# Value products of the first six token tiles taken from rows without the root of the norm, which a column out of PSUM applies afterwards

## The chip, the core and the metric

The kernel runs on one core of one Trainium2 chip. The metric is the device time of one execution in microseconds; the kernel before takes 2457.29 us, the median of three runs (2456.39 to 2457.72).

## What is computed

One layer of a hybrid encoder over 1088 tokens (1024 of a prompt and 64 of a running stream). The part that matters here is its beginning:

```python
xn = _rmsnorm(x, p['norm_mix_w'])
proj = xn @ p['w_in']
z, xbc, dt_raw, q, k, v, gate_ssm, gate_att = jnp.split(proj, ...)
...
def _rmsnorm(x, w):
    xf = x.astype(jnp.float32)
    y = xf * lax.rsqrt(jnp.mean(xf * xf, axis=-1, keepdims=True) + NORM_EPS)
    return (y * w.astype(jnp.float32)).astype(x.dtype)
```

The norm divides each token's row of 1024 numbers by the root of its mean square (a factor of the token) and multiplies it by a weight (a factor of the column). The projections `v` and `dt_raw` are taken first, then `q`, and the rest.

## The kernel before, in words

Activations lie transposed: features over the 128 partitions, in KT = 8 blocks, tokens along the free axis. Tokens go in nine tiles of 128 (the last of 64), and three neighbouring tiles make one part of `xn` (384, 384 and 320 tokens). Every product is taken in three matmuls of a rounded format, since a number is split into a high part (a cast, on ScalarE, ACT) and a low part (the difference, on VectorE, DVE): high x high, high x low, low x high. So a product over 1024 features is 8 x 3 = 24 matmuls.

The stage that is changed norms the nine tiles and takes the first half of the value products from them (two halves `f` of 256 columns, each with 16 columns of `dt`). Its steps for tile `x`: `fetch` loads the rows (`xc`); `squares` and `add_squares` square them and add eight blocks to two (`ns8`, shown as `ns` in the trace); `mean_square` lets TensorE (PE) sum over the partitions with a matrix of ones, which leaves each token's sum in all 128 partitions (`st`); `rstd_put` takes the root (three steps on ACT, two on DVE, into `nrs`); `weighted` and `scaled` multiply the rows by the negated weight and by `nrs`, which carries the other minus sign (`xr`); `put_high` and `put_low` write the parts `xn_hi` and `xn_lo`; `value_tile` takes the 24 products for one half into PSUM, evicts them with a copy on ACT (`vo`), stores them, and adds the bias of `dt` on DVE.

The order is set in two ways. What goes through `put` is chained by hand: each such instruction is issued after the one before it in the same engine's queue. The rest is ordered by the scheduler, within priorities. Value weights come in four blocks, two for each half, and are split on ACT and DVE as they land (`split_high`, `split_low`). For tile 0 the squares come first, `idle_products` keep PE busy with matmuls of ones in the meantime (9, then 8), then the mean, the root, the scaling and the split, and last the products. From tile 1 on `normed(x)` runs a tile ahead of the products.

Behind the stage come the projections `heads` with `project` (per block of 128 columns 24 matmuls for each of the three parts of `xn`; weights split by `weights`, line 147 and 148), and `steps`, which works on the `dt` columns on DVE and then takes sums with matmuls (lines 540 to 553).

Of the kernel before, what the change touches and what calls it, by code (L numbers as in the profile page):

```python
# [12 lines left out]
ALU = mybir.AluOpType  # L13
# [36 lines left out]
IDLE = (9, 8)  # L50
# [25 lines left out]
def hybrid_layer(ctx: ExitStack, tc: tile.TileContext, xT, xN, prm, cst, rope, wvd, win, wbs, wba, wout, wup, wdn,  # L76
# [181 lines left out]
    def value_tile(f, i, w2, dt=None, start=load, produce=product):  # L258
        m = 256 if dt is None else 272
# [3 lines left out]
        produce(ps, [(hi[:, k], lo[:, k], w2[k // 4][0][:, k % 4], w2[k // 4][1][:, k % 4]) for k in range(KT)])  # L263
        vo = staged("vo")[:, :256]
        with tc.high_priority(quick or ahead):
            S.copy(vo[:n], ps[:, :256])
            start(out=v[P * i : P * i + n, 256 * f : 256 * (f + 1)], in_=vo[:n])
            if dt is not None:
                V.tensor_tensor(out=dt[:n, i, 16 * f : 16 * f + 16], in0=ps[:, 256:],
                                in1=par[:n, O_DTB + 16 * f : O_DTB + 16 * f + 16], op=ALU.add)  # L270

    def values(f):
        w2 = [weights(win[B_V + 2 * f - 4 + u], 4, 256) for u in range(2)]
        for i in range(9):
            value_tile(f, i, w2)
            yield

    V.memset(dtw[TS:, 8], 0.0)
    with tc.tile_pool(name="nx", bufs=1) as nx:
# [21 lines left out]
        def tiles(x):  # L301
            for d, name, shape in ((s8, "ns8", [P, KT, P]), (xr, "xr", [P, KT, P]), (rs, "nrs", [P, P])):
                d[x] = nx.tile(shape, F32, name=name, tag=name, bufs=2)[..., : NORM[x]]
# [52 lines left out]

        def normed(x):
            rstd_put(x, ps[x])
            y = x + 1 if x + 1 < len(NORM) else None
            if y:  # L360
                tiles(y)
                for h in halves:
                    squares(y, h)
            if x == 1:
                scaled_half(x, halves[0])
                scaled(x, range(4, KT))
            else:
                scaled(x)
# [9 lines left out]
        def in_turns(*turns):  # L378
            turns = [(u, k) for u, ks in turns for k in ks]

            def produce(acc, terms):
                for i, (u, k) in enumerate(turns):
                    a_hi, a_lo, b_hi, b_lo = terms[k]
                    put(PE, PE.matmul, acc, a_lo if u == 2 else a_hi, b_lo if u == 1 else b_hi, start=i == 0,
                        stop=i == len(turns) - 1)

# [10 lines left out]
        xs.append(fetch(1))  # L397
        w += [raw_weights(wvd[2], 4, 272, extra), raw_weights(wvd[3], 4, 272, first)]
        w2 = [t[1:] for t in w]
        xs.append(fetch(2))  # L400
        load(out=par[:, O_FFN:], in_=prm[:, O_FFN:])
        tiles(0)
        tiles(1)
        a, b = halves
        all_k, low_k, high_k = range(KT), range(4), range(4, KT)
        idle_products(IDLE[0])
        squares(0, a)
        put(V, V.tensor_tensor, out=s8[0][:, b], in0=xs[0][:, b], in1=xs[0][:, b], op=ALU.mult)
        add_squares(0)
        ps = {0: mean_square(0, 2, put)}  # L410
        idle_products(IDLE[1])
        put(V, V.tensor_scalar_mul, par[:, O_MIX : O_MIX + KT], par[:, O_MIX : O_MIX + KT], -1.0)
        weighted(0, range(5), V)
        weighted(0, range(5, KT), S)
        rstd_put(0, ps[0])
        split_high(w[0])
        for h in halves:
            scaled_half(0, h)
            put_high(0, h)
        split_low(w[0])  # L420
        for h in halves:
            put_low(0, h)
        split_high(w[1])
        split_low(w[1])
        for h in halves:
            squares(1, h)
        add_squares(1)
# [3 lines left out]
        weighted(1, low_k, S)  # L431
        value_tile(0, 0, w2[:2], dtw, S.dma_start, in_turns((0, all_k), (1, low_k), (2, all_k), (1, high_k)))
        ps[1] = mean_square(1, 2, put)
        normed(1)
        with tc.issue_after(queue[S].ins):
            value_tile(1, 0, w2[2:], dtw, S.dma_start, in_turns((0, all_k), (2, all_k), (1, all_k)))
        for x in range(2, len(NORM) + 1):
            if x + 1 < len(NORM):
                xs.append(fetch(x + 1))
            if x < len(NORM):  # L440
                normed(x)
            for f in range(2):
                value_tile(f, x - 1, w2[2 * f : 2 * f + 2], dtw, S.dma_start, *[in_turns((0, all_k), (1, all_k), (2, all_k))] * (x == 2 and f == 0))
            if x == 3:
                load(out=con, in_=cst)
                for i, j, by in ((O_FFN, O_CW, -1.0), (O_CW, O_SN, 0.5), (O_SN, O_D, -0.5), (O_QN, O_FW, -1.0)):
                    put(V, V.tensor_scalar_mul, par[:, i:j], par[:, i:j], by)
# [3 lines left out]
    with tc.tile_pool(name="qk", bufs=1) as qk:  # L451
# [17 lines left out]
        def heads(blk0, wcol, to, plain):  # L469
# [3 lines left out]
            def block(j):  # L473
# [11 lines left out]
                return project(win[blk0 + j], evac)  # L485
# [1080 lines left out]
```

## Time and profile before

| what | value |
|---|---|
| median of three runs | 2457.29 us |
| profiled execution | 2457.47 us |
| its span on the core | 2455.7 us |
| PE, PE weight loads | 2426.9, 2351.5 us busy |
| DVE, ACT, GpSimd | 1600.6, 1137.8, 658.2 us busy |
| first value product, first projection product | 10.80, 73.51 us |

The profile is of one execution. A row of its timeline gives start, duration, engine, line, operation, output and inputs, the number of merged instructions, and in brackets the idle time ahead and what ended it. PEld is the loading of a matmul's fixed operand, PE the matmul itself, whose end is modelled. SP and ACT can issue DMAs. The span is the time from the first instruction to the last; the profiled execution is 1.8 us longer than its span.

### The profile page before, as it was taken

What the parts mean: (1) busy time and instruction counts of PE and PEld (TensorE: products, weight loads), DVE (VectorE), ACT (ScalarE), POOL (GpSimd) and SP (SyncE); (2) the same over time, 40 slices, a digit from 0 to 9 for tenths busy, and PEclk for the clock granted to TensorE, in tenths of its full rate; (3) what the DMA queues carried; (4) which work ended last, traced back from release to release, by engine and by line L of the source; (5) the groups of instructions that cost most, each with busy time, mean ns of one, the idle gap of its engine ahead of it and who ended that gap; (6) DMA issues with size and microseconds to landing.
All of it is one profiled execution on the core that took longest, in us unless ns stands there. A gap on an engine that the chain in (4) does not pass through costs nothing. (4 is left out here: it accounts for less than half of the span.)

```text
span 2455.7 us, 44603 instructions
## 1 busy us (share of the span) xinstructions
PE 2426.9 (99%) x16956; PEld 2351.5 (96%) x16956; DVE 1600.6 (65%) x2755; ACT 1137.8 (46%) x2497; POOL 658.2 (27%) x696
## 2 busy tenths in 40 slices
PE   9999999999999999999999999999999999999999
PEld 8999999999999999998899989999999999999999
DVE  7425254865777667546767785655776777777775
ACT  6334343644565555437664653224543434353441
POOL 0000000100011001004343333103376666655435
PEclk9999999999999999999999999999999999999999
DMA  4218158554353453345689765656234343467875
GB/s 173 82 57 293 58 216 257 139 166 129 118 162 110 129 169 106 97 159 183 201 266 323 224 197 178 191 176 189 70 117 147 116 153 116 133 209 205 223 176 163
DMA packets 269319, 403.55 MB, mean 164 GB/s; under 512 B 33296, under 2 KB 202000, under 8 KB 268976
## 3 DMA queue, kind: packets, MB, share of 16 engines
q1 hardware_dynamic: 258432, 385.06, 49.3%
q0 software_dynamic: 4608, 8.91, 2.4%
q10 hardware_dynamic: 6064, 6.72, 0.8%
q8 instruction: 133, 2.18, 0.4%
q14 instruction: 82, 0.67, 0.1%
HBM read 267.04 MB, written 133.56 MB: 163 GB/s over the span
## 5 line engine op out<-in xcount | busy, mean ns | idle before, releaser
L154 PE MATMUL mm<-xn_hi,w_hi 128*128 128x384 f32 (+1 forms) x1416 | 470.4, 332 | 0.9 <-DVE zr L590 0.9
L156 PE MATMUL mm<-xn_hi,w_lo 128*128 128x384 f32 (+1 forms) x1416 | 469.3, 331 | 0.5 <-DVE w_lo L148 0.5
L155 PE MATMUL mm<-xn_lo,w_hi 128*128 128x384 f32 (+1 forms) x1416 | 469.2, 331 | 0.0
L154 PEld LDWEIGHTS mm<-xn_hi,w_hi 128*128 128x128 f32 x1416 | 267.3, 189 | 4.8 <-issue 1.6
L156 PEld LDWEIGHTS mm<-xn_hi,w_lo 128*128 128x128 f32 x1416 | 267.4, 189 | 3.8 <-issue 2.0
L155 PEld LDWEIGHTS mm<-xn_lo,w_hi 128*128 128x128 f32 x1416 | 267.4, 189 | 2.6 <-issue 1.6
L148 DVE TENSOR_TENSOR w_lo<-w_f,w_hi 128x1024 fp32r<-128x1024 f32 x116 | 145.1, 1252 | 114.0 <-ACT w_hi L147 113.7
L1228 PE MATMUL mx<-n,wh 128*128 128x272 f32 x1076 | 206.2, 289 | 3.0 <-ACT u L1369 1.8
L1228 PE MATMUL mx<-m,w_hi 128*128 128x272 f32 x1010 | 192.3, 288 | 1.1 <-DVE down L1383 1.0
L147 ACT CAST w_hi<-w_f 128x1024 fp32r<-128x1024 f32 x116 | 121.3, 1048 | 145.8 <-PE mm L155 85.5
L1228 PEld LDWEIGHTS mx<-n,wh 128*128 128x128 f32 x1076 | 169.0, 188 | 4.1 <-ACT u L1369 2.5
L1228 PEld LDWEIGHTS mx<-m,w_hi 128*128 128x128 f32 x1010 | 158.7, 188 | 1.8 <-DVE down L1383 1.5
L1228 PE MATMUL mx<-n,wl 128*128 128x272 f32 x538 | 155.5, 289 | 0.0
L154 PE MATMUL mm<-b_hi,w_hi 128*128 128x384 f32 (+1 forms) x448 | 145.9, 327 | 0.8 <-DVE b_g L211 0.6
L156 PE MATMUL mm<-b_hi,w_lo 128*128 128x384 f32 (+1 forms) x448 | 145.0, 325 | 0.6 <-DVE w_lo L148 0.6
L1228 PE MATMUL mx<-m,w_lo 128*128 128x272 f32 x505 | 145.5, 288 | 0.0
L155 PE MATMUL mm<-b_lo,w_hi 128*128 128x384 f32 (+1 forms) x448 | 145.0, 324 | 0.0
L708 ACT ACTIVATE p_t<-sc,mx 128x1024 f32<-128x1024 f32 (+5 forms) x144 | 106.1, 738 | 78.9 <-DVE mx L699 37.2
L619 DVE SCALAR_TENSOR_TENSOR cc<-pre,par,cc 128x384 f32<-128x384 f32 (+1 forms) x216 | 126.5, 586 | 19.5 <-ACT cc L617 14.3
L607 POOL COPY pre<-pre 128x3 f32<-128x3 f32 x48 | 13.2, 276 | 456.9 <-ACT pre L608 346.8
L1019 ACT CAST w_hi<-ws 128x512 fp32r<-128x512 f32 (+1 forms) x62 | 37.6, 607 | 147.3 <-PE mx L1228 101.4
L154 PE MATMUL mx<-xn_hi,w_hi 128*128 128x384 f32 (+1 forms) x312 | 104.8, 336 | 0.8 <-DVE zr L590 0.8
(417 smaller groups left out, 6626.9 us busy)
## 6 DMA issues: line engine op xcount, KB each, us to landing
w_f<-in_win_dram SPq DMA_DIRECT2D x76, 512.0 KB, 4.0
w_f<-in_wup_dram SPq DMA_DIRECT2D x44, 512.0 KB, 3.8
hr<-q_sc SPq DMA_DIRECT2D x70, 272.0 KB, 4.8
bc<-a_sc SPq DMA_DIRECT2D x32, 512.0 KB, 5.8
q_sc<-hb SPq DMA_DIRECT2D x44, 272.0 KB, 2.3
gb<-q_sc SPq DMA_DIRECT2D x44, 272.0 KB, 3.8
x_sc<-cc SPq DMA_DIRECT2D x48, 192.0 KB, 2.3
q_sc<-gb SPq DMA_DIRECT2D x33, 272.0 KB, 2.2
```

Of the source, the lines that this page charges most:

```text
L147: S.copy(hi, w)
L148: V.tensor_tensor(out=lo, in0=w, in1=hi, op=ALU.subtract)
L154: PE.matmul(ps, a_hi, b_hi, start=i == 0, stop=False)
L155: PE.matmul(ps, a_hi, b_lo, start=False, stop=False)
L156: PE.matmul(ps, a_lo, b_hi, start=False, stop=i == n - 1)
L607: G.tensor_copy(pre[:, 0:3], tail)
L619: V.scalar_tensor_tensor(cc[:, :m], pre[:, i : i + m], cw(i), cc[:, :m], ALU.mult, ALU.add)
L708: act(p_t[:n, :nk], sc[c][:n, :nk], AF.Exp, bias=mx[:n, c : c + 1], accum_out=dst)
L1019: S.copy(hi, src)
L1228: PE.matmul(ps, w[x][:, c], b[y][:, k], start=start and k == t == 0, stop=k == nk - 1 and t == 2, skip_group_check=not start)
```

## The change

Tiles 0 to 5 (`RAW = 6`) are no longer normed before their value products. `raw(x)` weights the rows (half on ACT, half on DVE) and splits them; the products are taken from these rows. The squares and the mean follow beside, and the mean of tile `y` stands among the products of tile `y + 1`. A matmul of one row by one column turns the root from a row into a column in PSUM (`column`), a copy on DVE brings it to SBUF (`by`), and the eviction of tile `y`'s products, held in PSUM until then, multiplies by it, since in `v` tokens lie along the partitions. Tiles 6 to 8 are normed as before, ahead of their products. At the end `again(x)` multiplies the kept rows of tiles 3, 4, 5, 0, 1, 2 by their kept roots and splits them once more into `xn`, for the projections; the first projection block takes the parts in the order 2, 1, 0. The squares of the first tile go wholly to ACT, idle products are 14 in one run in place of 9 and 8, the four weight blocks are loaded ahead of the second tile's rows, value tiles 1 and later take high x high and high x low of the low and then of the high feature blocks first, then low x high, and the value stores are issued by SP in place of ACT.

In instructions: PE gets 6 column matmuls and 3 idle ones fewer, ACT 12 casts, 15 weightings and one square of 512 more and 18 DMA issues fewer, DVE 12 low parts, 9 products of 512 by the root, 21 weightings and 6 small copies more, and 36 fused weight-and-root products and one square fewer.

```diff
-IDLE = (9, 8)
+IDLE = 14
+RAW = 6
...
-    def project(block, evac):
+    def project(block, evac, order=(0, 1, 2)):
         w_hi, w_lo = weights(block, KT, P)
-        for (c, w), (hi, lo) in zip(WIDE, xn):
+        for x in order:
+            (c, w), (hi, lo) = WIDE[x], xn[x]
...
+    def value_out(f, i, ps, dt=None, start=load, by=None):
+        n = ps.shape[0]
         vo = staged("vo")[:, :256]
         with tc.high_priority(quick or ahead):
-            S.copy(vo[:n], ps[:, :256])
+            if by is None:
+                S.copy(vo[:n], ps[:, :256])
+            else:
+                act(vo[:n], ps[:, :256], AF.Copy, scale=by[:n])
             start(out=v[P * i : P * i + n, 256 * f : 256 * (f + 1)], in_=vo[:n])
...
+                    V.scalar_tensor_tensor(out, ps[:, 256:], by[:n], bias, ALU.mult, ALU.add)
...
+        def raw(x):
+            weighted(x, range(4), S)
+            weighted(x, range(4, KT), V)
+            for h in halves:
+                put_high(x, h)
+            for h in halves:
+                put_low(x, h)
+
+        def again(x):
+            for h in halves:
+                scaled_half(x, h)
+                put_high(x, h)
+            for h in halves:
+                put_low(x, h)
...
+        for x in range(1, len(NORM)):
+            y, z = x - 1, x + 1
+            if x + 3 < len(NORM):
+                xs.append(fetch(x + 3))
+
+            def means():
+                for u in [y] * (y < RAW) + [z] * (z == RAW):
+                    ps[u] = mean_square(u, 2, put)
+
+            def column():
+                pc = stat(P)[:, 0:1]
+                put(PE, PE.matmul, pc, rs[y][0:1], ones[0:1, 0:1], start=True, stop=True)
+                by[y] = nx.tile([P, 1], F32, name="by", tag="by", bufs=2)
+                column_at[y] = pc
+
+            to = [None, None]
+            at = (24 if x == 1 else 12, means), (18, column)
+            turns = (0, low_k), (1, low_k), (0, high_k), (1, high_k), (2, all_k)
+            to[0] = value_products(x, w2[:2], 272, in_turns(*turns, at=at[0]) if y < RAW else product)
+            if z < RAW:
+                tiles(z)
+                raw(z)
+            elif z < len(NORM):
+                normed(z)
+            if y < RAW:
+                rstd_put(y, ps[y])
+            if x < RAW:
+                add_squares(x)
+            if z < RAW:
+                stats(z)
+            if z + 1 == RAW:
+                tiles(RAW)
+                stats(RAW)
+                add_squares(RAW)
+            to[1] = value_products(x, w2[2:], 272, in_turns(*turns, at=at[1]) if y < RAW else product)
+            if y < RAW:
+                put(V, V.tensor_copy, by[y], column_at[y])
+                for f in range(2):
+                    value_out(f, y, held[f, y], dtw, by=by[y])
...
+        for x in (*range(3, RAW), *range(3)):
+            again(x)
...
-                return project(win[blk0 + j], evac)
+                return project(win[blk0 + j], evac, (2, 1, 0) if blk0 == B_Q and j == 0 else (0, 1, 2))
```

The order of PE at the very start, before (`w_hi` and `w_lo` are value weights, `xn_hi0` and `xn_lo0` the parts with tile 0, `st` a bank for sums):

```order
L296 MATMUL st_153<-ones_74 128x128 [waits DVE_49]
L299 MATMUL st_153<-ones_74 128x128 x8
L299 MATMUL st_167<-ns8_147,ones_74 128x128 [waits DVE_49]
L299 MATMUL st_167<-ns8_147,ones_74 128x128
L299 MATMUL st_170<-ones_74 128x128 x8
L299 MATMUL mx_217<-w_hi_125,xn_hi0_87 128x272 [waits Activation_49]
```

And in the changed kernel:

```order
L307 MATMUL st_153<-ones_74 128x128 [waits DVE_49]
L310 MATMUL st_153<-ones_74 128x128 x13
L310 MATMUL mx_191<-w_hi_125,xn_hi0_87 128x272 [waits Activation_49]
L310 MATMUL mx_191<-w_hi_125,xn_hi0_87 128x272 x3
L310 MATMUL mx_191<-w_hi_125,xn_lo0_88 128x272 [waits DVE_49]
```

The mean of tile 0 and the idle products behind it are gone from between, and the first product waits for ACT with nothing ahead of it but one run of idle products.

The order of DVE in the changed kernel in the pass for tile 5 (`ns8_689` holds the squares of tile 7, `xr_605` and `nrs_606` rows and root of tile 6, `nrs_481` the root of tile 4, `by_741` its column):

```order
L236 SCALAR_TENSOR_TENSOR nn0_682<-st_667,nn0_682 128x128
L237 SCALAR_TENSOR_TENSOR nrs_606<-nn0_682,nn1_683 128x128
L310 SCALAR_TENSOR_TENSOR xr_605<-xc_448,par_72,nrs_606 128x128 x8
L310 TENSOR_TENSOR ns8_689<-ns8_689 128x512
L310 TENSOR_TENSOR ns8_689<-ns8_689 128x256
L310 TENSOR_TENSOR xn_lo2_92<-xr_605,xn_hi2_91 128x4x128 x2
L236 SCALAR_TENSOR_TENSOR nn0_711<-st_664,nn0_711 128x128
L237 SCALAR_TENSOR_TENSOR nrs_481<-nn0_711,nn1_712 128x128
```

The nearest piece of before, where one tile is normed at a time:

```order
L234 SCALAR_TENSOR_TENSOR nn0_492<-st_423,nn0_492 128x128
L235 SCALAR_TENSOR_TENSOR nrs_406<-nn0_492,nn1_493 128x128
L299 SCALAR_TENSOR_TENSOR xr_405<-xc_394,par_72,nrs_406 128x128 x8
L299 TENSOR_TENSOR ns8_499<-ns8_499 128x512
L269 TENSOR_TENSOR dtt_98<-mx_521,par_72 128x16
L299 TENSOR_TENSOR ns8_499<-ns8_499 128x256
L299 TENSOR_TENSOR xn_lo1_90<-xr_405,xn_hi1_89 128x4x128 x2
```

A second root, that of tile 4, now stands behind tile 6's whole chain, and PE's column for tile 4 stands behind that root.

The order of DVE ahead of the projections in the changed kernel (`w_lo_1108` is the low part of the first projection's weights; `xr_386`, `xr_480`, `xr_579` are the kept rows of tiles 3, 4 and 5):

```order
L310 TENSOR_TENSOR xr_386<-xr_386,nrs_387 128x512 x2
L279 TENSOR_TENSOR dtt_98<-mx_866,par_72 128x16
L310 TENSOR_TENSOR xn_lo1_90<-xr_386,xn_hi1_89 128x4x128 x2
L310 TENSOR_TENSOR xr_480<-xr_480,nrs_481 128x512 x2
L279 TENSOR_TENSOR dtt_98<-mx_910,par_72 128x16
L310 TENSOR_TENSOR xn_lo1_90<-xr_480,xn_hi1_89 128x4x128
L149 TENSOR_TENSOR w_lo_1195<-w_f_1193,w_hi_1194 128x1024
L310 TENSOR_TENSOR xn_lo1_90<-xr_480,xn_hi1_89 128x4x128
L310 TENSOR_TENSOR xr_579<-xr_579,nrs_580 128x512 x2
L279 TENSOR_TENSOR dtt_98<-mx_943,par_72 64x16
L149 TENSOR_TENSOR w_lo_1288<-w_f_1286,w_hi_1287 128x1024
L149 TENSOR_TENSOR w_lo_1108<-w_f_1106,w_hi_1107 128x1024
```

And before, where `w_lo_1055` is the one of the first projection:

```order
L299 TENSOR_TENSOR xn_lo2_92<-xr_770,xn_hi2_91 128x4x64 x2
L269 TENSOR_TENSOR dtt_98<-mx_868,par_72 128x16
L269 TENSOR_TENSOR dtt_98<-mx_897,par_72 128x16
L148 TENSOR_TENSOR w_lo_1142<-w_f_1140,w_hi_1141 128x1024
L269 TENSOR_TENSOR dtt_98<-mx_926,par_72 64x16
L148 TENSOR_TENSOR w_lo_1235<-w_f_1233,w_hi_1234 128x1024
L148 TENSOR_TENSOR w_lo_1055<-w_f_1053,w_hi_1054 128x1024
```

Ten operations on kept rows now stand ahead of the same three splits, and those of tiles 0, 1 and 2 behind them, ahead of `steps`. From the second half of the first projections on, at about 100 us, the order is that of before on every engine.

More of the change, by code (lines that the diff above doesn't have):

```diff
@@ L361, in normed @@
                 tiles(y)
[L362 to L368, printed above, removed]
+                stats(y)
+            scaled(x)
             if y:
@@ L430, in hybrid_layer @@
             split_low(t)
[L431 to L441, printed above, removed]
+        ps, by, held, column_at = {}, {}, {}, {}
@@ new lines, in hybrid_layer @@
+        for f in range(2):
+            held[f, 0] = value_products(0, w2[2 * f : 2 * f + 2], 272, in_turns(
+                (0, low_k), (2, low_k), (1, low_k), (0, high_k), (2, high_k), (1, high_k)))
+        tiles(1)
+        raw(1)
+        stats(1)
+        add_squares(0)
+        for x in range(1, len(NORM)):
[32 more added lines that the diff above has]
+                put(V, V.tensor_copy, by[y], column_at[y])
+                for f in range(2):
+                    value_out(f, y, held[f, y], dtw, by=by[y])
```

61 lines of the change are left out of this document (33 added, 28 removed).

## The prediction

> **What bounds the kernel now.** I read the page first, then busy time by stretch, then what TensorE waits for at the start, then the rows there one by one.
>
> ```profile
> span 2455.7 us, 44603 instructions
> ...
> PE 2426.9 (99%) x16956; PEld 2351.5 (96%) x16956; DVE 1600.6 (65%) x2755; ACT 1137.8 (46%) x2497; POOL 658.2 (27%) x696
> ```
> ```profile
> 0.00:100.00 100.00, 94.54 (x661) 91.01 (x662) 68.23 (x183) 50.87 (x111) 0.20 (x4) 1.00 0.42 146
> ```
> TensorE (PE) is busy 2426.9 of 2455.7 us, so only what it waits for, or is given more of, moves the end. The change rewrites the normalisation and value products, which fill about the first 73 us, and the order on every engine is the same again from about 100 us on. What lies behind is shifted as one block. In the first 100 us PE is idle for 5.5 us by its matmul rows and 9.0 by its weight loads (PEld). I count by the loads, since a matmul's end is modelled. The pieces of that idle time after the first value product:
>
> ```profile
> 10.80 0.55 PEld L299 LDWEIGHTS mx<-w_hi,xn_hi 128*128 128x128 f32 x4 [0.48 <-ACT xn_hi L299]
> 12.40 0.55 PEld L299 LDWEIGHTS mx<-w_hi,xn_hi 128*128 128x128 f32 x4 [1.05 <-ACT w_hi L299]
> 15.49 0.52 PEld L299 LDWEIGHTS st<-ns,ones 128*128 128x128 f32 x4 [0.54 <-PE mx L299]
> 20.40 0.55 PEld L299 LDWEIGHTS mm<-w_hi,xn_hi 128*128 128x128 f32 x4 [1.41 <-ACT xn_hi L299]
> 21.45 0.55 PEld L299 LDWEIGHTS mm<-w_hi,xn_hi 128*128 128x128 f32 x4 [0.25 <-ACT xn_hi L299]
> 27.68 0.19 PEld L154 LDWEIGHTS mx<-w_hi,xn_hi 128*128 128x128 f32 x1 [0.45 <-ACT xn_hi L299]
> 28.79 0.52 PEld L312 LDWEIGHTS st<-ns,ones 128*128 128x128 f32 x4 [0.56 <-DVE ns L299]
> ```
> The first value product starts at 10.80. Behind it PE loses 1.05 + 0.54 + 1.41 + 0.25 + 0.45 + 0.56 = 4.26 us; from 29 us on it runs without a break to the first projection product at 73.51:
>
> ```profile
> 16.92 1.07 PEld L299 LDWEIGHTS mx<-w_hi,xn_lo 128*128 128x128 f32 x8
> 17.93 1.07 PEld L299 LDWEIGHTS mx<-w_lo,xn_hi 128*128 128x128 f32 x8
> ```
> ```profile
> 48.54 0.61 PE L312 MATMUL st<-ns,ones 128*128 128x128 f32 x4
> ...
> 49.11 0.29 PE L154 MATMUL mx<-w_hi,xn_hi 128*128 128x272 f32 x1
> ...
> 73.51 0.34 PE L154 MATMUL mm<-xn_hi,w_hi 128*128 128x384 f32 x1
> ```
> Eight products take 17.93 - 16.92 = 1.01 us, 0.126 each. A mean of squares with the product behind it takes 49.11 - 48.54 = 0.57, so it adds 0.445. The stage by this count: 10.80 + 9 tiles x 48 x 0.126 (54.4) + 8 means x 0.445 (3.6) + 4.26 = 73.1, where the trace has 73.5. The count holds to 0.4 us, so I count the changed kernel in the same way.
>
> **The change part by part.** *Start.* Tile 0 no longer waits for squares, mean and root before its first product. What is then late next?
>
> ```profile
> L280 ACTq DMA_DIRECT2D par<-in_prm_dram x1: 419/419/419, 0.7 to 0.7; - x1
> ...
> DMA to landing us min/median/max: 3.1/3.1/3.1
> ```
> ```profile
> L141 SPq DMA_DIRECT2D w_f<-in_wvd_dram x1: 432/432/432, 1.6 to 1.6; - x1
> ...
> DMA to landing us min/median/max: 6.1/6.1/6.1
> ```
> ```profile
> 3.72 0.63 ACT L296 ACTIVATE ns<-xc 128x512 f32<-128x512 f32 x1 [1.25 <-DMA xc<-in_xN_dram]
> 6.47 0.99 ACT L299 ACTIVATE xr<-xc,par 128x128 f32<-128x128 f32 x3 [2.12 <-DVE par L299]
> 8.63 1.08 ACT L299 CAST w_hi<-w_f 128x1088 fp32r<-128x1088 f32 x1
> 10.13 1.22 ACT L299 CAST xn_hi<-xr 128x512 fp32r<-128x512 f32 x2 [0.42 <-DVE xr L299]
> ```
> ```profile
> 4.41 0.69 DVE L296 TENSOR_TENSOR ns<-xc 128x512 f32<-128x512 f32 x1 [3.25 <-DMA xc<-in_xN_dram]
> 6.47 1.07 DVE L299 TENSOR_SCALAR xr<-xc,par 128x128 f32<-128x128 f32 x5
> 10.62 1.28 DVE L299 TENSOR_TENSOR w_lo<-w_f,w_hi 128x1088 fp32r<-128x1088 f32 x1
> ```
> The rows of tile 0 land at 3.7 and 4.4, the parameters at 3.8; weighting (0.2 a piece on DVE, 0.3 on ACT) and the two casts (1.22) are done by about 6.2. The first weights, third in the queue as before, land at 1.6 + 6.1 = 7.8. Their cast (1.08) comes last: PE starts at 8.95 instead of 10.80, **1.85 saved**. So the DMA takes the place of the root. On ACT the other three casts follow, with two squares of 0.6 between, and are done by 13.0; on DVE the four low parts (1.28, each behind its cast) end at 10.2, 11.8, 13.3 and 14.5. PE, at 0.126 a product, needs them at 10.0, 11.8, 13.3 and 14.8, so it waits 0.3 in all and finishes tile 0 at about 15.3.
>
> *Tiles 1 to 4.* A tile takes PE 48 x 0.126 + 0.445 = 6.5, with the new column 6.6. ACT has four weightings (1.2), two casts (1.2), two squares (1.2), and two evictions and three steps of the root, whose rows stand below (0.75 and 1.1): 5.5. DVE has four weightings, low part, adds and root, 0.8 + 1.3 + 1.15 + 0.65, and three small rows: 4.3. Both are done in time, so **the waits of 4.26 become 0.3**, 4.0 saved.
>
> *Added PE work.* The mean of tile 0 now stands among the products: 0.445. Six column matmuls (one row in, 128x1 out) have no row like them. Below I set nothing, above half a mean, 0.22; I take 0.15, 0.9 for six: a tiny operand, but two changes of what PE loads. Together **1.3**. Three idle products of 17 go from a stretch in which PE waits anyway: nothing.
>
> *Tile 5, where tile 6 is normed the old way.* Here the chain gets longer. In the pass for tile 5, PE's order has the means of tiles 4 and 6 after 12 products, then 30 products, the mean of tile 7, and tile 4's column. DVE's order in between is root of 6, eight weightings, the adds of 7, low part of 6, root of 4. The same links in the trace of before:
>
> ```profile
> 46.85 0.37 ACT L266 COPY vo<-mm 128x256 f32<-128x256 f32 x1 [0.63 <-PE mm L156]
> ...
> 49.19 0.37 ACT L231 ACTIVATE nn<-st,eps_t 128x128 f32<-128x128 f32 x1 [0.58 <-PE st L312]
> ```
> ```profile
> 50.27 0.29 DVE L234 SCALAR_TENSOR_TENSOR nn<-st,nn 128x128 f32<-128x128 f32 x1 [1.22 <-ACT nn L233]
> ...
> 50.92 2.19 DVE L299 SCALAR_TENSOR_TENSOR xr<-xc,par,nrs 128x128 f32<-128x128 f32 x8
> 53.03 0.68 DVE L299 TENSOR_TENSOR ns<-ns 128x512 f32<-128x512 f32 x1
> ...
> 54.18 1.29 DVE L299 TENSOR_TENSOR xn_lo<-xr,xn_hi 128x512 fp32r<-128x512 f32 x2
> ```
> From the means' issue, 0: PE has issued both at 0.9 and reaches tile 7's mean 30 x 0.126 = 3.8 later, at 4.7. DVE can start tile 6's root 1.1 after ACT has the mean (50.27 - 49.19; about 1.1 + 1.1 = 2.2), weights from 2.9 to 5.0 (53.03 - 50.92), and has the adds (54.18 - 53.03) by 6.2: PE waits 1.5. Mean done at 6.6; the low part (two at 0.6) takes until 7.3 and tile 4's root 0.65 (50.92 - 50.27), so the column can start at 7.9: another 1.3. **2.8 added.** Before, the same chain ended in time because only one tile was in it. The later tiles have room again: PE reaches their columns after the roots.
>
> The stage: -1.85 - 4.0 + 1.3 + 2.8 = **-1.7**; the projections start near 71.4 by the count, 71.8 on the trace's scale.
>
> *Projections.* Six tiles are scaled and split again: 12 scalings and 12 low parts on DVE at 0.6 each, 14.6 us, and 12 casts on ACT. DVE reaches them after tile 8's low part, whose cast stands behind ACT's eviction of tile 6 (PE ends tile 6 at 62.5 by the count; cast and low part make it 63.7). Ahead of the low part of the first projection's weights are ten such operations (6.1) and three weight splits:
>
> ```profile
> 72.32 2.36 DVE L148 TENSOR_TENSOR w_lo<-w_f,w_hi 128x1024 fp32r<-128x1024 f32 x2 [0.46 <-ACT w_hi L147]
> ...
> 75.33 0.31 DVE L532 TENSOR_SCALAR dtt<-dtt 128x288 f32<-128x288 f32 x1 [0.51 <-ACT de L522]
> ...
> 84.44 0.09 DVE L537 MEMSET da<- 64x32 f32 x1
> 89.53 0.46 DVE L541 TENSOR_SCALAR nacum<-st 128x288 f32<-128x288 f32 x1 [5.00 <-PE st L540]
> ```
> At 1.2 a split that is 3.6, with 0.6 for small rows and hand-overs 74.0. PE needs it after three products, at 71.9, and stands: before, it had six products without that operand to bridge, now two and one that itself waits 0.2. **2.3 added.** The last three tiles' parts (7.8, with the hand-overs) then put the time-step chain, 75.33 to 84.5 in the trace, with a weight split in it at 83.4 to 93.9. Before, it had 5.0 us to spare; PE's order now has its first matmul 4.8 us later (120 products ahead of it instead of 92, at 0.17), at 93.7 by the count. **0.3 added**, and no room left. The tokens of tiles 0 to 2 are not late themselves: their low parts are there at 82.6, PE asks at 84.5.
>
> The move of the 18 value stores from ACT's to SP's queue, and the later rows, I set at nothing: next in SP's queue are row tiles with a pass to spare.
>
> Sum: -1.7 + 2.3 + 0.3 = **+0.9 us**. Of the profiled execution (2457.47, 1.8 beyond its span) that makes 2458.4; the median of the runs shown is 0.2 lower, so I forecast **2458.2**. About 0.2%, 4.9 us, is what a measurement of this kernel can tell from no change.
>
> **A rule on the clock.** PE's idle products keep it busy while it waits:
>
> ```profile
> L299 PE MATMUL st<-ones 128*128 128x128 f32 x16 | 3.6, 421 | 0.0
> ```
> ```profile
> L299 PE MATMUL st<-ones 128*128 128x128 f32 x6 | 1.0, 299 | 0.0
> ```
> In 1.5 to 5.2 us such a matmul takes 421 ns, after 9.9 us 299 and less: PE works at about half rate first, although the granted clock reads 1.00 in both. It became fast after 3.4 us of unbroken work from 6.4 on; the 4.2 us from 1.05 had not been enough. Now one run of 14 products (28 matmuls at 0.213, to about 7) is followed by 2 us of nothing. The Trainium skill, "TensorE: Matmul & The Clock Gate", Part 1, says that the array runs at half clock until one free-running window of about 3.4 us has been busy, and again after an idle window of that length. By that rule 6 us of work contain a whole window most times and the gap is too short to lose it; where the windows lie badly, the value products start at half rate. The trace agrees with the 3.4 us, and no run here shows a gap of 2 us.
>
> **The rivals.** *Cold start.* If PE is at half rate from 8.95, each such us costs 0.5, less the 0.3 it waits anyway: 3.4 to 6.8 us make 1.4 to 3.1, 2459.6 to 2461.3. For it: the first stretch of 4.2 us did not do. Against: 6 us do more. Chance 0.12.
>
> *The two late chains aren't late.* If ACT and DVE run ahead of my count, the 2.8 and 2.6 go: 2452.8, just inside no change. Both are in the fixed order with durations that repeat; 0.07.
>
> *The second split makes DVE the bound.* With no room left before the time-step chain, each 1% on the 30 us of DVE from 63.7 to 93.9 costs 0.3. The 24 hand-overs between DVE and ACT there are the doubtful part: at 0.17 us more each it is 4.1 later, 2462.3, slower by over 0.2%. For it: DVE's share is 65% already, and PE has to wait in the forecast. Against: hand-overs in the rows above are 0.05 to 0.15, which I counted. Chance 0.06.
>
> *The start doesn't move,* because the weights land later than in the old queue: 1.85 comes back, 2460.1. They stand at the same place in it; 0.03.
>
> **How the numbers follow.** The forecast, with 0.72, spans 2456.4 to 2460: columns -0.9 to +0.4, each late chain 0.4 either way, landing 0.5. With the cold start and part of the others the range is 2455.8 to 2461.5. Faster by over 0.2% needs the second rival and more: 0.03. Slower: the third, and the worst of the first: 0.08. Same: 0.89.
>
> **What would show it.** First value product at 8.9, waiting for the cast of the weights; no wait over 0.4 us from there to 45; then about 1.5 us for tile 7's adds and 1.3 for tile 4's root near 49 to 51; 2 us for the weights' low part at the first projection; under 1 us at the first matmul of the time steps. It is wrong if value products come 0.25 us apart before 15 us, or if TensorE waits in a place not named here.

## The result, and the profile after

The changed kernel takes 2460.14 us (median of 13 runs, 2455.14 to 2462.83), the kernel before 2456.47 (13 runs beside it, 2452.36 to 2459.41). The ratio is 1.0016 with a 95% interval of 1.0009 to 1.0023: 0.16% slower, 2.2 to 5.7 us, and so within the 0.2% that counts as no change here, though the interval leaves out 1 and its upper end is a little beyond 0.2%. The profiled execution took 2458.27.

The page of the changed kernel, its span and the busy time of the engines; then its first 100 us as one stretch, with TensorE's granted clock after the busy times:

```profile
span 2456.5 us, 44662 instructions
...
PE 2429.5 (99%) x16962; PEld 2355.9 (96%) x16962; DVE 1601.2 (65%) x2766; ACT 1152.0 (47%) x2525; POOL 661.7 (27%) x696
```
```profile
0.00:100.00 100.00, 93.16 (x641) 90.67 (x642) 73.86 (x189) 59.50 (x130) 0.20 (x4) 0.97 0.41 144
```

TensorE is 1.4 us less busy in that stretch (93.16, before 94.54), and **the granted clock is 0.97 where it was 1.00**. These are the two things to explain. First the waits: weight loads between 8 and 80 us with idle time ahead of them, its length and releaser in brackets (the columns at 29, 36 and 43 us, with 0.15 like the one at 22.40, are left out):

```profile
8.90 0.55 PEld L310 LDWEIGHTS mx<-w_hi,xn_hi 128*128 128x128 f32 x4 [2.17 <-ACT w_hi L310]
...
22.40 0.29 PEld L310 LDWEIGHTS st<-ones,nrs 1*128 1x128 f32 x2 [0.15 <-issue]
...
52.06 0.52 PEld L325 LDWEIGHTS st<-ns,ones 128*128 128x128 f32 x4 [1.55 <-DVE ns L310]
53.80 0.29 PEld L310 LDWEIGHTS st<-ones,nrs 1*128 1x128 f32 x2 [1.21 <-DVE nrs L237]
```
```profile
78.14 0.19 PEld L157 LDWEIGHTS mm<-xn_hi,w_lo 128*128 128x128 f32 x1 [1.71 <-DVE w_lo L149]
```

The six waits of before are gone, and the three new ones of over 1 us stand where they were forecast. Yet the first projection product, with which the stage ends, starts at 75.93 instead of 73.51. The same stretch cut into windows of 3.41 us shows why:

```profile
6.27:9.68 3.41, 1.43 (x12) 1.24 (x11) 1.47 (x3) 1.93 (x3) 0.00 (x0) 1.00 1.01 402
9.68:13.09 3.41, 3.41 (x16) 3.33 (x16) 2.95 (x3) 3.41 (x5) 0.00 (x0) 0.50 1.05 405
13.09:16.51 3.42, 3.42 (x29) 3.42 (x29) 3.33 (x9) 2.95 (x8) 0.00 (x0) 1.00 1.05 402
...
50.64:54.06 3.42, 1.06 (x7) 0.79 (x6) 3.35 (x9) 1.73 (x5) 0.00 (x0) 1.00 0.00 0
54.06:57.47 3.41, 3.41 (x17) 3.40 (x17) 3.26 (x13) 2.72 (x8) 0.00 (x0) 0.50 0.19 63
```

Read the first number behind the window's length (TensorE busy) against PEclk of the *next* row. A window in which TensorE was busy for 1.43 of 3.41 us (42%), or 1.06 (31%), is followed by one at clock 0.50, and that by one at 1.00. Each of these half-clock windows costs half its length, 1.7 us, as TensorE has work throughout. It is to be seen in single products, four to a row:

```profile
11.30 1.11 PE L310 MATMUL mx<-w_hi,xn_hi 128*128 128x272 f32 x4
12.21 1.07 PE L310 MATMUL mx<-w_hi,xn_lo 128*128 128x272 f32 x4
...
14.11 0.66 PE L310 MATMUL mx<-w_hi,xn_lo 128*128 128x272 f32 x4
14.61 0.66 PE L310 MATMUL mx<-w_lo,xn_hi 128*128 128x272 f32 x4
```

12.21 - 11.30 = 0.91 for four, 0.23 each; behind 13.1 it is 0.50 for four, 0.125 each. The second surprise is the column:

```profile
22.06 0.41 PE L310 MATMUL mm<-w_hi,xn_lo 128*128 128x272 f32 x2
22.40 0.38 PE L310 MATMUL st<-ones,nrs 1*128 1x1 f32 x2
22.71 1.02 PE L310 MATMUL mm<-w_hi,xn_lo 128*128 128x272 f32 x6
...
29.35 0.38 PE L310 MATMUL st<-ones,nrs 1*128 1x1 f32 x2
```

From one column to the next it is 29.35 - 22.40 = 6.95 us, where 6.5 was counted for a tile without one: 0.45 a column, not 0.15.

### The profile page after: what moved, and what is told of

Same layout as the page of the kernel before. It is cut to its first block, busy times and chain, and to the rows that moved or that the text cites. A ratio compares the mean times of both kernels' runs of the same rounds, so it can differ in the third digit from the quotient of the medians.

```text
span 2456.5 us, 44662 instructions
## 1 busy us (share of the span) xinstructions
PE 2429.5 (99%) x16962; PEld 2355.9 (96%) x16962; DVE 1601.2 (65%) x2766; ACT 1152.0 (47%) x2525; POOL 661.7 (27%) x696
## 4 chain that ended last, share of the span: by engine, by line
PE 90%; DMA 4%; DVE 2%; ACT 1%; issue 1%; SPq 1%; POOL 0%; DVEq 0%; POOLq 0%; ACTq 0%
PE mx L1291 18%; PE mm L157 12%; PE mm L155 12%; PE mm L156 12%; PE mm L1291 7%; PE mx L155 4%; PE mx L157 4%; PE mx L156 4%; PE po L805 3%; PE sc L758 2%; PE sc L757 1%; PE mx L1350 1%; PE pt L786 1%; DMA kl_t<-k_st 1%; PE yi L921 1%; PE ye L927 1%
## 5 line engine op out<-in xcount | busy, mean ns | idle before, releaser
L670 POOL COPY pre<-pre 128x3 f32<-128x3 f32 x48 | 13.7, 285 | 453.3 <-ACT pre L671 345.3
```

## The experiments

All but one were timed in five rounds beside the kernel before; figures like 1.0011 (1.0001 to 1.0021) are ratios to it with their 95% intervals. Where traces are compared, "lateness at 100 us" is the start of the first product after 100 us against the same product of the profiled kernel before (+3.7 us in the changed kernel).

### More idle products

```diff
-IDLE = 14
+IDLE = 20
```


> Six idle products more (20 instead of 14), which fill 1.3 us of the 2.0 us in which TensorE stands before its first value product; nothing else is changed. Theory (clock by windows): TensorE's granted clock is set in fixed windows of 3.4 us; a window of which less than half is busy is followed by one at half clock. In the changed kernel 6.3 to 9.7 is 42% busy and 9.7 to 13.1 shows 0.50; now it is about 80% busy, the clock reads 1.00 there, the products keep 0.125 us each, and 1.7 us are saved less at most 0.4 us of new waits for low parts of weights: first column at about 20.8 instead of 22.4, whole 2458.5 against 2460.1. Rival (the onset of dense products draws the throttle, whatever comes before): the stretch at 0.50 stays at 9.7 to 13.1, column at 22.4, whole unchanged at 2460.1.

The window ahead of the first products, and the next, of this kernel (columns as above):

```profile
5.43:8.85 3.42, 2.43 (x22) 2.23 (x20) 1.29 (x2) 1.56 (x3) 0.00 (x0) 1.00 0.95 327
8.85:12.26 3.41, 3.02 (x21) 2.80 (x22) 2.63 (x3) 3.41 (x6) 0.00 (x0) 1.00 1.02 402
```

With the window ahead of the products 71% busy, the clock stays at 1.00; the second half-clock window, which this edit doesn't touch, is still there (53.2 to 56.6, at 0.50). The first column comes at 21.47 instead of 22.40, although the first product started 0.28 later (9.18) and, at full speed, waits 0.28 for a low part of the weights: 1.5 us gained at that place. Whole: 1.0011 (1.0001 to 1.0021), 2459.38; the gain by ratios, about 1.2 us, is inside the two intervals. The theory's sign is in the trace, the rival is out: the products begin as densely as before, and draw no throttle. Nor does it hang on one execution: of the four traces with 14 idle products three have a half-clock window at the start (the early mean's hasn't), of the six with 20 none.

### Tile 6's mean half a pass earlier

```diff
-                for u in [y] * (y < RAW) + [z] * (z == RAW):
+                for u in [y] * (y < RAW):
                     ps[u] = mean_square(u, 2, put)
...
             def column():
...
+                if z + 1 == RAW:
+                    ps[RAW] = mean_square(RAW, 2, put)
```


> The mean of tile 6 half a pass earlier (behind tile 3's column, not beside tile 4's mean), so that root 6 no longer stands in one chain with root 4. Theory (chain order): the waits for tile 7's adds (1.55 by the weight loads) and tile 4's root (1.21) fall under 0.4 each, window 50.6 to 54.1 stays over half busy, and with it the half clock at 54.1 to 57.5 goes: 2.8 + 1.7 = 4.5 less, first projection product at 71.5 instead of 75.9; the wait for the weights' low part there stays near 1.7; whole 2455.6. Rival (DVE is the bound from there on): the projection starts 4.5 earlier and waits that much longer, 6 us, for its low part; the whole stays at 2460.1.

The same pass of this kernel, in windows, and TensorE's waits at the first projection:

```profile
48.93:52.34 3.41, 3.41 (x27) 3.27 (x27) 3.15 (x11) 2.33 (x7) 0.00 (x0) 1.00 0.00 0
52.34:55.76 3.42, 3.42 (x30) 3.42 (x29) 3.39 (x12) 2.13 (x5) 0.00 (x0) 1.00 0.23 77
```
```profile
70.94 0.19 PEld L155 LDWEIGHTS mm<-xn_hi,w_hi 128*128 128x128 f32 x1 [0.45 <-ACT w_hi L148]
72.62 0.19 PEld L155 LDWEIGHTS mx<-xn_hi,w_hi 128*128 128x128 f32 x1 [1.39 <-ACT xn_hi L310]
73.70 0.19 PEld L157 LDWEIGHTS mm<-xn_hi,w_lo 128*128 128x128 f32 x1 [0.90 <-DVE w_lo L149]
```

Both waits at tile 5 are gone (0.43 is left at the mean that was moved, at 42.24), the windows there are full, and no half clock follows. At the first projection 2.74 us are waited for instead of 1.71, so about 1 comes back, as a part of the rival said. Whole: 0.9999 (0.9988 to 1.0010), 2455.83; against the changed kernel 4.2 us less by the ratios. (In the profiled execution the half clock at the start is missing too, so its lateness of -0.8 at 100 us holds about 1.5 that isn't the edit's.) Of all single edits this is the only one whose ratio is back at 1.

### The column out of 128 rows

```diff
+        unit = nx.tile([P, 1], F32, name="unit")
+        put(V, V.memset, unit, 1.0 / P)
...
-                put(PE, PE.matmul, pc, rs[y][0:1], ones[0:1, 0:1], start=True, stop=True)
+                put(PE, PE.matmul, pc, rs[y], unit[:, 0:1], start=True, stop=True)
```


> The column out of all 128 rows: nrs (the same row in every partition) against a column of 1/128, instead of one row against a 1x1 one. The column now costs TensorE 0.50 us (22.18 to 23.06 for three products' pitch of 0.126 and it). Theory (a load of one row has to wait for the array to drain): it falls to about 0.25, half a mean, six columns 1.5 us less, tile pitch 6.7 instead of 6.95, whole 2458.6. Rival (the price is the change between the two kinds of matmul, as in the 0.44 of a mean): 0.45 to 0.5 as before, whole 2460.1.

TensorE's matmuls around two columns of this kernel:

```profile
22.04 0.42 PE L310 MATMUL mm<-w_hi,xn_lo 128*128 128x272 f32 x2
22.30 0.28 PE L310 MATMUL st<-unit,nrs 128*128 128x1 f32 x2
22.43 0.99 PE L310 MATMUL mm<-w_hi,xn_lo 128*128 128x272 f32 x6
...
28.96 0.28 PE L310 MATMUL st<-unit,nrs 128*128 128x1 f32 x2
```

A tile with its column now takes 28.96 - 22.30 = 6.66 us: the column costs 0.16 instead of 0.45, though 128 times as many rows go in. So the price was not that of a small matmul, nor of the change between the two kinds, which is the same in both; it was the one row. Whole: 1.0011 (0.9999 to 1.0022), 2457.90; six times 0.29 = 1.7 us in the trace, 1.2 by the ratios, a difference inside the two intervals.

### Tile 3's second scaling early

```diff
+            if x == RAW:
+                again(3)
             to[1] = value_products(x, w2[2:], 272, in_turns(*turns, at=at[1]) if y < RAW else product)
...
-        for x in (*range(3, RAW), *range(3)):
+        for x in (4, 5, *range(3)):
             again(x)
```


> Tile 3's second scaling and split stand in the pass of tile 6, ahead of tile 5's column, where DVE waits 3.3 us for TensorE; the other five stay at the end. Theory (DVE's queue ahead of the first projection's weights): their low part comes 2.5 us earlier, the wait of 1.71 falls under 0.3, whole 2458.4. Rival (the root of tile 8 now stands behind tile 3's casts, and TensorE waits at tile 8 instead, about 1.5 us): 2460.

It didn't gain: 1.0025 (1.0011 to 1.0038), 2459.37, slower than the kernel before and, with overlapping intervals, not told apart from the changed kernel by the whole. In the first 100 us of its trace it loses, and neither theory had the reason. Windows around tile 5's waits in this kernel:

```profile
49.70:53.12 3.42, 1.28 (x9) 0.86 (x7) 3.35 (x9) 1.89 (x5) 0.00 (x0) 1.00 0.00 0
53.12:56.53 3.41, 3.20 (x14) 3.18 (x15) 3.26 (x12) 2.57 (x8) 0.00 (x0) 0.50 0.07 25
56.53:59.95 3.42, 3.42 (x17) 3.42 (x17) 2.88 (x9) 1.69 (x5) 0.00 (x0) 0.50 0.16 52
```

Here the window behind the wait began 0.2 us before TensorE did, so that it was busy for 3.20 of 3.41 us, and **the half clock lasted a second window**. What share of busy time brings the clock back isn't settled: a half-clock window 82% busy (425.9, four tiles) was also followed by a second, but one of 86% (428.7, 20 idle products) and one of 89% (73.7, POOL but tile 3) were not.

The wait for the weights' low part was 2.22 instead of 1.71. The theory about DVE's queue was not put to the test by this: into the place of tile 3's operations moved those of tile 0, and as in the changed kernel six scalings and four low parts of rows stand ahead of the split that TensorE waits for. DVE's last ones:

```profile
76.05 1.28 DVE L310 TENSOR_TENSOR xr<-xr,nrs 128x512 f32<-128x512 f32 x2
...
77.33 2.34 DVE L149 TENSOR_TENSOR w_lo<-w_f,w_hi 128x1024 fp32r<-128x1024 f32 x2
```

Behind that wait, at 80.4, a further half-clock window followed. The two more than in the changed kernel make 3.4 us; lateness at 100 us is 2.9 higher, 6.6.

### The three mends together, and with four tiles instead of six

The first is the three edits with an effect of their own (20 idle products, the early mean, 128 rows); the second is the same with four tiles.

```diff
-IDLE = 14
+IDLE = 20
-RAW = 6
+RAW = 4
```

> Three edits that each had their effect alone, together: 20 idle products, the mean of tile 6 half a pass earlier, the column out of 128 rows. Theory (the costs add): against the changed kernel's 2460.1, 1.5 for the half-clock window at 9.7, 4.2 for the waits at tile 5 with their half-clock window, 1.7 for six columns, and about 1 given back at the first projection, whose weights' low part waits for DVE: first column at 20.7, first projection product at about 68.5, whole 2453.7, ratio to before 0.9989. Rival (the projections are bound by DVE and the release of the value weights): what is saved ahead of 70 is waited for behind it, over 3 us there, and the whole is 2456 or more.

> The same with four tiles from rows without the root instead of six: two columns fewer (0.4), and four second scalings and four second low parts fewer on DVE (4.9 us), four casts fewer on ACT. Theory (DVE and ACT behind tile 8 are what makes the first projection wait): the waits there, 1.7 in the changed kernel and 2.7 with tile 6's mean early, fall under 1.2; whole about 1.5 under the run with six tiles, 2452. Rival (the changeover to tiles normed first, which now stands at 29 to 43 us where DVE and ACT have less room, brings its waits of 2.8 us back and with them a half-clock window): 2456 to 2458.

The windows at the first projection, of the first kernel:

```profile
70.10:73.52 3.42, 1.57 (x7) 1.05 (x8) 3.42 (x7) 1.57 (x4) 0.00 (x0) 1.00 0.86 281
73.52:76.93 3.41, 3.41 (x14) 3.41 (x14) 3.33 (x7) 1.22 (x2) 0.00 (x0) 0.50 0.55 178
```

With the mends the first projection starts at 70.18, 5.8 us earlier than in the changed kernel, but 2.74 us are waited for there, and a half-clock window follows: the rival's 3 us and 1.7 more. The run with the early mean alone has the same waits, but there they fall into two windows (62% busy in the emptier) and no half clock follows; which it is depends on where the windows lie in an execution. Lateness at 100 us is 0.0 instead of 3.7; whole 0.9997 (0.9987 to 1.0007), 2454.02, no difference from before. With four tiles the waits there are 2.6 (0.41 and 2.19), not under 1.2, and the half clock (at 74.3) is there too; whole 1.0002 (0.9992 to 1.0013), 2457.86. At the changeover only 0.63 and 0.15 are waited for, so the rival's waits aren't there either, though the whole fits its 2456 to 2458. The four scalings and low parts fewer bought nothing, and couldn't at this place: those of tiles 3, 0 and 1 now stand ahead of the split, again six scalings and four low parts.

### No idle products

```diff
-IDLE = 14
+IDLE = 0
```


> The changed kernel without any idle product: TensorE does nothing until its first value product at 8.9. Theory (windows of 3.4 us; full speed comes only after a window that is busy through): products come 0.25 us apart from 8.9 until the end of the first full window, that is for 3.4 to 6.8 us, and the first column stands 1.7 to 3.4 later than the 20.8 of a start at full speed, at 22.5 to 24.2. Rival (the idle products do nothing; half clock is only drawn by a drop in the load): 0.125 apart from the start, column at 20.8, no stretch under 1.00.

TensorE's products at the change of pace:

```profile
12.52 1.07 PE L310 MATMUL mx<-w_hi,xn_lo 128*128 128x272 f32 x4
13.43 0.67 PE L310 MATMUL mx<-w_lo,xn_hi 128*128 128x272 f32 x4
13.93 0.66 PE L310 MATMUL mx<-w_hi,xn_hi 128*128 128x272 f32 x4
```

0.23 a product up to 13.4, 0.125 behind it: half speed for 4.7 us from 8.73 on, until the first window in which it was busy throughout (10.00 to 13.41) was over. The first column is at 22.72, inside the theory's 22.5 to 24.2. The granted clock reads 1.00 in all of this: **at the start of a kernel the profile's clock doesn't show the slow pace, the distance between matmuls does.** (The trace's list of clock states begins only at 13.4 us here; where it has none, the views show 1.00.) One run, 2461.50.

### The second scalings on POOL

All twelve scalings on POOL (GpSimd), behind each tile's root, on top of the three mends; then the same without the mends; then tile 3, or tiles 3 to 5, back on DVE.

```diff
         def scaled_half(x, h):
...
-            put(V, V.tensor_tensor, out=xr[x][:, h], in0=xr[x][:, h], in1=by, op=ALU.mult)
+            put(G, G.tensor_tensor, out=xr[x][:, h], in0=xr[x][:, h], in1=by, op=ALU.mult)
...
         def again(x):
             for h in halves:
-                scaled_half(x, h)
                 put_high(x, h)
...
             if y < RAW:
                 rstd_put(y, ps[y])
+                for h in halves:
+                    scaled_half(y, h)
```


> The three mends, and the twelve second scalings on POOL (GpSimd), right behind each tile's root, instead of on DVE at the end. POOL does nothing in the first 100 us; a like operation of 128x512 takes it 1.36 to 1.42 us in the profile of before, so 17 us in all between 17 and 65. Theory (DVE's queue, full from 66 to 77 in the run with the three mends, sets the waits of 2.7 us at the first projection, which empty a window and so cost a half-clock window of 1.7 too): DVE has 7.7 us less, the waits fall under 0.8 in all, no stretch at 0.50 near 73, time steps' first matmul 4 us earlier; whole 2454.0 - 3.6 = 2450.4, ratio 0.998. Rival (the weights' split waits for TensorE to release the value weights, whatever DVE does): waits stay at 2 or more, whole 2453 to 2454.

> The changed kernel with nothing but the twelve second scalings moved to POOL. Theory (DVE's queue): the wait of 1.71 at the first projection falls under 0.5; the half-clock windows at the start and at 54 stay; first projection product still near 75.9, whole 2460.1 - 1.4 = 2458.7. Rival (release of the value weights): wait 1.5 or more, whole 2460.

The first: 0.9990 (0.9981 to 0.9999), 2453.99. The wait at the first projection is still 2.78, for the weights' high part, whose cast now stands behind twelve casts on ACT (6.4 us). The rival's numbers hold, but its reason, the release of the value weights, isn't shown by that: DVE's queue ahead of the weights' splits didn't get shorter either, since all twelve low parts moved ahead of them:

```profile
66.71 7.31 DVE L310 TENSOR_TENSOR xn_lo<-xr,xn_hi 128x512 fp32r<-128x512 f32 x12 [0.28 <-ACT xn_hi L310]
```

And a new wait of 2.58 us at 43.8, with a half-clock window behind it, came from here, DVE's four adds and POOL's two scalings beside them:

```profile
39.48 4.25 DVE L310 TENSOR_TENSOR ns<-ns 128x512 f32<-128x512 f32 x4
```
```profile
39.70 3.02 POOL L310 TENSOR_TENSOR xr<-xr,nrs 128x512 f32<-128x512 f32 x2 [3.49 <-DVE nrs L237]
```

The second: 1.0007 (0.9997 to 1.0016), 2458.69, as its theory said for the whole; the rival's 2460 lies within the interval too. Its trace can't be set beside the others, so its waits stay unread.

```diff
+POOLED = (0, 1, 2, 4, 5)
...
-            put(G, G.tensor_tensor, out=xr[x][:, h], in0=xr[x][:, h], in1=by, op=ALU.mult)
+            put(*((G, G.tensor_tensor) if x in POOLED else (V, V.tensor_tensor)), out=xr[x][:, h], in0=xr[x][:, h], in1=by, op=ALU.mult)
```

(and `(0, 1, 2)` in the last run; tiles not in `POOLED` are scaled in `again`, as in the changed kernel)

> As the run with the mends and POOL, but tile 3's scaling back on DVE at the end. There POOL scaled tile 3 from 39.7 to 42.7, while DVE's four adds (two sets) took 4.25 us from 39.5 on; in the run without POOL four such adds take 2.3. Theory (POOL and DVE slow each other down while both run such operations): with POOL still between 37 and 43 the adds take 2.3 us, TensorE's wait of 2.58 at 43.8 falls under 0.7, its window stays over half busy, and the half clock at 43.7 to 47.1 goes: column of tile 4 at 49.3 as without POOL instead of 52.75; whole 1.5 to 3.5 under that run's 2454.0. Rival (the adds are slow for another reason, squares of ACT that come late): adds stay near 4.2 us, wait over 2.

> POOL scales tiles 0, 1 and 2 only (21 to 36 us); tiles 3, 4 and 5 on DVE at the end, whose queue there has six scalings instead of twelve. Theory: no wait over 0.7 up to the first projection, which starts near 70; there 1 to 2 us of waiting (2.7 with all twelve on DVE; the weights' casts on ACT aren't behind all twelve second casts as with all on POOL); whole 2451 to 2452.5. Rival (what DVE gains, ACT's twelve casts and the release of the value weights take): waits of 2.7 there as before, whole 2454.

DVE's same four adds with tile 3 taken from POOL:

```profile
39.29 1.14 DVE L311 TENSOR_TENSOR ns<-ns 128x512 f32<-128x512 f32 x2
40.84 1.15 DVE L311 TENSOR_TENSOR ns<-ns 128x512 f32<-128x512 f32 x2 [0.41 <-ACT ns L311]
```

Four adds take 2.29 us alone and 4.25 beside POOL; the wait falls to 1.06 (not under 0.7), no half clock follows, and tile 4's column is at 49.60 instead of 52.75. Whole 0.9988 (0.9979 to 0.9996), 2453.31, only 0.5 to 0.7 better, which the intervals don't tell from nothing: at the first projection 3.71 us are now waited for, with a half-clock window at 73.7 that the first of these runs hadn't. With tiles 3 to 5 on DVE: 0.9984 (0.9975 to 0.9994), **2451.68, the fastest of all**: 0.16% under the kernel before, with an interval that leaves out 1 but within the 0.2% that counts as no change, and clear of the changed kernel. This although 2.73 us are still waited for at the first projection and a half-clock window follows at 73.1. The wait there is the same 2.7 as with the three mends, and so is what stands ahead of the split on DVE: tiles 3 to 5, six scalings and four low parts; the scalings that went to POOL had stood behind it. No run whose trace can be read made that queue shorter (with twelve or ten scalings on POOL, twelve low parts stand there), so what sets the wait (DVE's queue, ACT's casts, the release of the value weights) was not told apart and stays open.

## Why the prediction was right or wrong

The forecast of no change by the bound of 0.2% held, and 2460.1 is inside 2455.8 to 2461.5. The forecast of +0.9 was 2.8 us short of +3.7, and the number of the rival given 0.12, the cold start, is part of what happened. Term by term, from the traces:

| term | forecast, us | measured, us |
|---|---|---|
| first value product | 8.95 | 8.90 |
| waits up to tile 4 | 0.3 | none (0.28 in the run at full clock) |
| six columns | 0.9 | 2.7 (0.45 each) |
| waits at tile 5 | 1.5 + 1.3 | 1.55 + 1.21 |
| half-clock window at 9.7 | rival, 1.4 to 3.1 | 1.7 |
| half-clock window at 54.1 | not named | 1.7 |
| first projection product | 71.4 | 75.93 |
| wait for the weights' low part | 2.3 | 1.71 |
| first matmul of the time steps | 0.3 | none seen |

With the three differences the count closes: 71.4 + 1.8 + 1.7 + 1.7 - 0.3 = 76.3, where the trace has 75.93. On the trace's scale the forecast was 71.8, which makes 76.7, 0.8 too late; and at 100 us the same differences, with 0.6 less for the low part and 0.3 for the time steps, would make 0.9 + 4.0 = 4.9 where it is 3.7. So about 1 us of saving is in none of the terms, and that the range held in spite of 5.2 us of missing cost is in part luck. The time steps are late by as much on both engines: DVE's chain starts at 87.6 instead of the 83.4 counted (where 74.0 + 7.8 would be 81.8; the rest of that step is not shown), TensorE's first matmul comes at 97.97 instead of 93.7.

**The columns: a step of the sum mis-sized.** I set "above half a mean, 0.22" as their bound and reasoned "a tiny operand, but two changes of what PE loads". The runs: 0.45 with one row in, 0.16 with 128. The two changes cost what I took; the bound was drawn by size, and the price isn't one of size. The Trainium skill, "TensorEngine Tiling (Array Packing)", in Tiling Modes, says that a change of the tiling mode drains TensorE. The two columns differ in just that the one loads a single row, and the run with 128 rows agrees; that a load of one row counts as another mode no run shows by itself.

**The cold start: the wrong rival was made small.** Its size came true, its way didn't: the value products don't start cold. TensorE's first recorded clock is 1.00 at 6.27, behind a window busy throughout, and it lost that through the gap. I wrote that "the gap is too short to lose it", taking from the rule that a whole window must be idle. In the traces a window less than about half busy is enough: 42% and 31% here, 41% in the kernel before at 402 us, 46% in the run with four tiles. At 45% (the run with the early mean, 4.6 to 8.0) it did not come, at 50% (before, 1419.5) neither, but at 59% (the run with 128 rows, 50.5) it did, so the edge is not sharp by this measure of busy time. Over the twelve traces used, every one of 36 windows under 45% busy is followed by a half-clock one, 6 of 29 between 45 and 60%, and none that was fuller. The Trainium skill, "TensorE: Matmul & The Clock Gate", Part 1, gives the window as 3413 ns, free-running, and the return to half clock after an idle one. The length agrees: the two half-clock windows in the first 100 us start 44.38 us apart, 13.0 times that, and those of every trace used lie on such a grid, whose phase differs from execution to execution. That an idle window is needed doesn't agree.

**The waits at tile 5: sizes right, consequence missed.** 2.76 us of waiting inside one window empty it, and the clock behind it costs 1.7 on top. Waits of over about 1.9 us in one window had this surcharge every time (they leave less than 45% of it busy), and the forecast had two such places in its own sum (2.8 at tile 5, 2.3 at the projection) without it.

**"What lies behind is shifted as one block".** It is, from 100 us (+3.7) to 395 (+3.6). At 400 to 405 TensorE waits for tiles of q and k from memory, in the kernel before for 4.5 us with a half-clock window behind it:

```profile
402.33:405.74 3.41, 1.41 (x5) 0.99 (x6) 0.00 (x0) 0.78 (x2) 0.18 (x1) 1.00 1.13 259
405.74:409.15 3.41, 3.41 (x12) 3.41 (x12) 3.10 (x5) 1.25 (x3) 0.00 (x0) 0.50 0.71 186
```

In the changed kernel's execution it waited 1.6 there, with none, and was 0.8 *ahead* at 420. Two later half-clock windows (at 1423 and 2392, not in the profile before) put it back by 1.4 and 2.2, smaller differences take 2.0 of that away, and at the end it is +0.8. So two single profiles differ by 0.8 where the medians differ by 3.7. Over the runs the medians follow the lateness at 100 us:

| run | lateness at 100 us, us | by the ratio, us |
|---|---|---|
| the change | +3.7 | +3.9 |
| 20 idle products | +2.8 | +2.7 |
| early mean | -0.8 | -0.2 |
| column of 128 rows | +2.2 | +2.7 |
| tile 3 early | +6.6 | +6.1 |
| three mends | 0.0 | -0.7 |
| three mends, four tiles | +0.2 | +0.5 |
| mends and POOL | +2.5 | -2.5 |
| POOL but tile 3 | +2.0 | -2.9 |
| POOL for tiles 0 to 2 | 0.0 | -3.9 |

(The second number is the ratio less 1, times 2456.) In the first seven rows they agree within 0.7, closer than the intervals (some 2.5 us either way) would lead one to expect. The granted clocks of whole executions agree with the count: their mean is 0.9965 in 13 of the changed kernel and 0.9981 in 33 of the kernel before (those of 2448.7 to 2460.6 us beside the first experiments), each clock listed to three digits. The 0.0015 between them are 3.7 us of 2456, as much as lies between the medians: **without its extra half-clock windows the change would be even, not slower.** This is a count, with no run of its own.

In the three rows with POOL the end is 4 to 5 us better than the first 100 us say. Between 395 and 2440 us their traces have less idle time of TensorE (13.7 to 14.4 us, 17.1 in the run with the three mends) and one or two half-clock windows where that run has three. That makes 5.0 to 6.5 us less, where these executions are 5.0 to 5.6 better behind 100 us than the run with the three mends; but each is one execution, and why they wait less stays open.

What was right: the six waits vanish, DMA bounds the start at 8.9, the chain through two roots at tile 5 and the split behind the second scaling are late where the orders said.

## What to carry to other kernels

Price a wait on TensorE by the window that it falls in: one that empties more than half of some 3.4 us costs 1.7 us more, and a gap ahead of a dense stretch can be filled with idle products up to its end. A small matmul that reads one partition is not cheap; give it the full 128 rows where the data is there in each of them. When the granted clock of a stretch isn't 1.00, look at that before the waits. And when an edit is meant to shorten a queue, look in its trace at what moved up into the place.

## What the runs showed of the hardware

- Half clock comes in windows of 3.41 us: behind each of 36 that were less than 45% busy, behind 6 of 29 that were 45 to 60% busy, behind none that was fuller. It mostly lasts one window; of seven half-clock windows that weren't quite full, two (82% and 94% busy) were followed by a second, five (86 to 98%) were not.
- The start of a program is at half speed with the clock shown as 1.00: 0.23 us a product until 13.4 us without idle products.
- A matmul of one row in and one column out cost 0.45 us, of 128 rows 0.16.
- DVE's additions of two operands in memory take nearly twice as long while POOL multiplies such operands (four adds 4.25 us against 2.29), and so do its products of rows with the weight (four of 128x128 in 1.82 us at 22.84 with all scalings on POOL, 0.87 at 21.76 with none).
